# Differential attention in a hybrid layer: prompt scores as two fp32r passes over stacked high and low halves

## The chip, the cores and the metric

One core of a Trainium2 chip runs the kernel. The metric is the device time of one execution in microseconds (us); the time of before is the median of three runs. The profile is one further execution, recorded by the hardware profiler.

## What is computed

One layer on 512 prompt tokens and 64 sample tokens (a second request with a cache of 256 tokens): a gated delta rule (GDN) and a differential attention side by side, then a memory attention, then a feed-forward block. All tensors are fp32. The change touches the differential attention only. Each of its 4 heads has a query and a key of 128 numbers, two components of 64:

```python
s = jnp.einsum('bqhcd,bkhcd->bhcqk', qi.astype(jnp.float32), kf) * scale     # c: the two components
visible = k_pos[None, :] < ((pi // CHUNK + 1) * CHUNK)[:, None]              # chunks of 64
p = jax.nn.softmax(jnp.where(visible, s, -jnp.inf), axis=-1)
a = p[:, :, 0] - lam * p[:, :, 1]
o = jnp.einsum('bhqk,bkhe->bqhe', a, vf)
```

The new keys and values of prompt and sample are outputs too. The GDN works in chunks of 128 tokens (four of the prompt, and a fifth for the sample); for each it inverts a triangular system (`gdn_prep`) and then carries a state through the chunks (`gdn_scan`).

## The kernel before

The layer is kept transposed (features on the 128 partitions, 576 tokens along a row). A projection (`project`, L169) makes 128 output features for all tokens: a first half of 256 prompt tokens and a second half of 256 prompt and 64 sample tokens, each into one PSUM bank of the tag `pr`, of which there are three (L75). Weights and activations stand split into a high and a low fp32r part; a half takes 16 matmuls (8 of 512 columns, 8 of 256) or 24 (of 320 columns). An `evac` function empties the bank, and the bank is free for another half when its last reader is done.

In the order of the program: projections of the GDN, `gdn_prep` of chunk c+1 ahead of `gdn_scan` of chunk c (L905), then for each head h `diff_project(h)` (L946: query, key and value), one step of the sample's scan, and `diff_head(h)` (L996: the sample's tile t = 4 first, then the prompt's tiles 0 to 3). The tile framework's scheduler then orders each engine's instructions by priority and readiness, with buffers handed out as they come free; nothing but that sets the order here. It puts the projections of the attention among the steps of the GDN, and those of the next head among the scores of this one.

`gdn_prep` has a loop of levels (L755): on PE a turn of `Y` and a product of `Dt` and `B` into a bank `g0` or `g1`; ACT copies `X` (L763); DVE makes `Y` (L764); PE multiplies them; DVE updates `Y` (L771) and `Dt` (L772); then the next level. Chunks 0 to 3 have five levels between the first and the last 64 rows, and a closing part (L773 to 784); the sample's chunk 4 has five. `normed` (L798) and the row norms use a power on POOL (`rpow`, L207), for which DVE waits.

Buffers are of tags with one or two slots (`small`, L92). `At0`/`At1` and `Y0`/`Y1` have one slot each and serve the chunks of even and odd number in turn, the sample's chunk 4 those with 0. `kd`, `vb`, `X`, `KQ` and `zr` have two. `zr` is the fp32 buffer into which a projection's bank is emptied.

Of `diff_project`, before: the query's bank is copied into `qz` (L194, L195, L957), component c into its 64 rows of a buffer of its own whose other 64 rows are zero (L942, L943, memsets on POOL); keys go to `kdT` in the large buffer `u5`, transposes of keys and values through a bank `ba` to the output and to `vtm`, in `u5` as well. A score of `diff_head` is one fp32 matmul of `qz[:, c]` (128 columns of queries) against `kdT` (nk = 128, 256, 384 or 512 keys for t = 0 to 3); in the profile each fp32 matmul is two instructions. The SyncE queue (SP) issues all loads and stores in order, weights (`raw`, three slots, L157) among them; an issue that must wait holds those behind it.

Of the kernel before, what the change touches and what calls it, by code (L numbers as in the profile page):

```python
# [8 lines left out]
F32 = mybir.dt.float32  # L9
F32R = mybir.dt.float32r  # L10
AF = mybir.ActivationFunctionType
ALU = mybir.AluOpType
# [3 lines left out]
P = 128  # L16
D = 1024
KT = 8
SEQ = 512
DEC = 64  # L20
T = SEQ + DEC
HALVES = ((0, 256), (256, T - 256))
PAST = 256
# [14 lines left out]
def hybrid_layer_kernel(  # L38
# [9 lines left out]
    nc = tc.nc  # L48
    V, A, G = nc.vector, nc.scalar, nc.gpsimd
# [17 lines left out]
    cp = ctx.enter_context(tc.tile_pool(name="cp", bufs=1))  # L67
# [32 lines left out]
    def bank(tag="ba"):  # L100
        return ps.tile([P, 512], F32, tag=tag, name=nm(tag), bufs=BANKS[tag])
# [4 lines left out]
    def mm(out, lhsT, rhs, start=True, stop=True, pin=False, skip_group_check=False):  # L106
        i = nc.tensor.matmul(out, lhsT, rhs, start=start, stop=stop, skip_group_check=skip_group_check)  # L107
        if pin:
            tc.keep_in_program_order(i)
# [11 lines left out]
    e2, e3, e4, e5 = [pair(i) for i in (2, 3, 4, 5)]  # L121
# [71 lines left out]
    def add_to(dst, b, more):  # L193
        A.copy(dst, more)  # L194
        V.tensor_tensor(dst, b, dst, ALU.add)  # L195
# [244 lines left out]
    for typ in (1, 0, 2):  # L440
# [3 lines left out]
        for h in range(H):  # L444
# [8 lines left out]
            n = SOFF + DEC  # L453
# [40 lines left out]
    for a0, n in HALVES:  # L494
        b = bank("pr")
# [7 lines left out]
    b = bank()  # L503
# [50 lines left out]
    for j in range(3):  # L554
        b = bank()
# [374 lines left out]
    nlam = const([P, 1], "nlam")  # L930
    V.scalar_tensor_tensor(nlam, le[:, 1:2], -LAM0, le[:, 0:1], ALU.add, ALU.subtract)

    od, kdT = e3[:, 0], e5[:, 0]
    vtm = view(e5, 1, 4, 4 * P)
    vs = cp.tile([P, 4, P], F32, tag="vs", name="vs")
    cv2 = view(e3, 1, 4, 4 * P).rearrange("p (i b) n -> p i b n", i=2)
    ckT, cvv = cv2[:, 0].rearrange("p b (c n) -> p (b c) n", n=PAST), cv2[:, 1]

    qz = [cp.tile([P, 2, T], F32, tag=f"qz{i}", name=f"qz{i}") for i in range(2)]
    with tc.issue_after(behind_keys[0]), tc.issue_after(behind_keys[1]):  # L940
        for q2 in qz:
            G.memset(q2[64:, 0, :], 0.0)  # L942
            G.memset(q2[:64, 1, :], 0.0)  # L943
        G.memset(vs[64:], 0.0)

    def diff_project(h):  # L946
        hs = slice(h * P, (h + 1) * P)
        for kind, base in (("q", 2056), ("k", 2568), ("v", 3080)):
            def evac(b, a0, n, more):
                ts_ = slice(a0, a0 + n)  # L950
                if kind == "q":
                    for c in range(2):
                        R = slice(64 * c, 64 * c + 64)
                        if more is not None:
                            add_to(qz[h % 2][R, c, ts_], b[R], more[R])
                        else:
                            (A.copy if c else V.tensor_copy)(qz[h % 2][R, c, ts_], b[R])  # L957
                    return
                d = small("zr", [P, 320])[:, :n] if kind == "v" else kdT[:, h, ts_]
                if more is not None:  # L960
                    add_to(d, b, more)
                else:
                    V.tensor_copy(d, b)
                bt = bank()
                for t in range(2):
                    tr(bt[:, t * P : (t + 1) * P], d[:, t * P : (t + 1) * P])
                if a0:
                    tr(bt[:DEC, 256:384], d[:, 256:])
                src, t2 = bt[:, :256].rearrange("p (t d) -> p t d", t=2), slice(a0 // P, a0 // P + 2)
                if kind == "v":  # L970
                    A.copy(vtm[:, t2, hs], src)
                    if a0:
                        A.copy(vs[:DEC, h, :], bt[:DEC, 256:384])
                else:
                    ko = small("ko", [P, 3, P])
                    A.copy(ko[:, :2], src)
                    nc.sync.dma_start(o_dk_p[0, 0, a0 : a0 + 256, h, :].rearrange("(t p) d -> p t d", p=P), ko[:, :2])
                    if a0:
                        A.copy(ko[:DEC, 2], bt[:DEC, 256:384])
                        nc.sync.dma_start(o_dk_s[0, 0, :, h, :], ko[:DEC, 2])  # L980

            project(weights(w2, base + h * P), xs, evac)
        nc.sync.dma_start(o_dv_p[0, 0, :, h, :].rearrange("(t p) d -> p t d", p=P), vtm[:, :, hs])
        nc.sync.dma_start(o_dv_s[0, 0, :, h, :], vs[:DEC, h, :])

    def diff_cache():
# [9 lines left out]
    def diff_head(h, between):  # L996


        hs = slice(h * P, (h + 1) * P)
        so, co = tiny([P, 5], "ta"), tiny([P, 5], "ta")  # L1000
        on = small("an", [P, 5, P])
        for t in (4, 0, 1, 2, 3):
            if t == 1:
                between()
            q0 = QT[t][0]
            nk = q0 + P if t < 4 else PAST + DEC
            nb = (nk + P - 1) // P
            pr = []
            mx, l = tiny([P, 2], "ta"), tiny([P, 2], "ta")
            for c in range(2):  # L1010
                b = bank(f"g{c}")
                qq = qz[h % 2][:, c, q0 : q0 + P]
                if t < 4:
                    mm(b[:, :nk], qq, kdT[:, h, :nk])
                    V.memset(b[:64, nk - 64 : nk], -1e30)
                else:
                    mm(b[:, :PAST], qq, ckT[:, h, :])
                    mm(b[:, PAST:nk], qq, kdT[:, h, SEQ:T])
# [4 lines left out]
                pr.append(p)  # L1023
# [12 lines left out]
            for kb in range(nb):  # L1036
                if t < 4:
                    vv = vtm[:, kb, hs]
# [41 lines left out]
    for w, out in ((w_mem_k, o_mk), (w_mem_v, o_mv)):  # L1080
        dst = tokens
        for f in range(2):
            fs = slice(512 * f, 512 * f + 512)
            bs = [bank("pr") for _ in range(2)]
            for kc in range(4):
                wt = split_weights(w[0, 256 * kc : 256 * kc + 256, fs], [P, 2, 512])
                for k in (2 * kc, 2 * kc + 1):
                    for t in range(2):
                        ts_ = slice(t * P, (t + 1) * P)
                        for j, (wi, x) in enumerate(((0, mh), (0, ml), (1, mh))):  # L1090
                            mm(
                                bs[t], x[:, k, ts_], wt[wi][:, k % 2, :],
                                start=(k == 0 and j == 0), stop=(k == KT - 1 and j == 2),
# [6 lines left out]
            if out is o_mk:  # L1100
                for i in range(2):
                    b = bank()
# [79 lines left out]
    for k2 in range(KT // 2):  # L1182
        b = bank()
# [6 lines left out]
    for h in range(H):  # L1190
# [15 lines left out]
        for t, (q0, _) in enumerate(QT):  # L1206
            t0, n = TT[t]
            kk, kl = (mkT, mkl) if t < 4 else (cmT, cml)
            b = bank(("gs", "g0", "g1")[t % 3])
# [9 lines left out]
            p = small("p0", [P, 512])  # L1219
# [15 lines left out]
        for i in range(2):  # L1235
            b, b2 = bank(("g0", "gs")[i]), bank(("g1", "ba")[i])
# [8 lines left out]
            j = 2 * (h % 2) + i  # L1245
# [328 lines left out]
    for m in range(KT):  # L1574
# [3 lines left out]
        if m in (3, 4):  # L1578
            t = m - 3
# [43 lines left out]
```

## Time and profile before

| | |
|---|---|
| time, median of 3 runs | 987.23 us (987.15 to 987.32) |
| the profiled execution, its own time | 987.2 us |
| its span in the trace | 985.5 us (1.7 us lie around it) |
| granted TensorE clock, mean | 0.997 |
| PE, DVE, ACT, POOL busy | 98%, 71%, 54%, 6% of the span |
| from chunk 2's second level of the GDN to the end of chunk 4 | 189 to 248 us |
| scores of the differential attention | 250 to 348 us |

PE's busy time counts a matmul from its start to its modelled end, so neighbours overlap; what one costs in a dense stretch is read from start to start, or from the end of one to the end of the next. Names of buffers stand without their numbers in the profile: `g` is a bank g0 or g1, `u` any of the large buffers.

### The profile page before, as it was taken

Reading aid. Unit: us, or ns where it says so; the run is one execution under the profiler, and the core shown is the slowest. Engines: PE = TensorE matmul, PEld = TensorE weight load, DVE = VectorE, ACT = ScalarE, POOL = GpSimd, SP = SyncE. Lnnn points to the kernel's source line nnn. Section 1 sums busy time; section 2 is a strip of 40 time slices with the busy share of each in tenths; the row PEclk is TensorE's granted clock in tenths of the full one; section 3 lists DMA queues with packets and bytes.
Section 4 is the critical chain, followed back from the end, with each engine's and each line's share of the span. In section 5 each row is a group of like instructions: output and inputs, shape, how many; then the busy total and the mean of one; then the engine's idle time right before and its main releaser. Section 6 shows DMA issues by size and latency. Waiting matters only on the chain.

```text
span 985.5 us, 16923 instructions
## 1 busy us (share of the span) xinstructions
PE 968.5 (98%) x6403; PEld 891.2 (90%) x6403; DVE 699.7 (71%) x1570; ACT 530.1 (54%) x1194; POOL 58.8 (6%) x127
## 2 busy tenths in 40 slices
PE   9999999999999999999999999999999999999996
PEld 7989899898888878999999999999999999999996
DVE  6666787877676676666557977657867779978674
ACT  7545575344656665444445657665544445555444
POOL 3341011101000000000000000000000000000000
PEclk9999999999999999999999999999999999999998
DMA  7432340103222647333111414222222223223202
GB/s 212 129 119 65 90 138 23 43 23 103 81 68 68 203 131 227 95 94 99 44 44 58 127 54 127 86 86 86 86 87 86 86 86 86 86 86 86 65 23 96
DMA packets 121714, 90.75 MB, mean 92 GB/s; under 512 B 5564, under 2 KB 112206, under 8 KB 121122
## 3 DMA queue, kind: packets, MB, share of 16 engines
q1 hardware_dynamic: 121266, 89.03, 30.9%
q8 instruction: 50, 0.82, 0.3%
q10 hardware_dynamic: 368, 0.66, 0.2%
q14 instruction: 30, 0.25, 0.1%
HBM read 79.93 MB, written 9.75 MB: 91 GB/s over the span
## 4 chain that ended last, share of the span: by engine, by line
PE 83%; DVE 4%; issue 3%; POOL 2%; DMA 2%; ACT 2%; POOLq 0%; ACTq 0%; SPq 0%; DVEq 0%
PE pr L107 51%; PE g L107 12%; PE ba L107 10%; PE gs L107 6%; PE ba L113 3%; PE g L113 1%; POOL tg L208 1%; DMA r<-in_w_ff_dram 1%; DVE p L457 1%; DVE wl L162 0%; DMA grow<-gdram 0%; DMA raw<-in_w_ff_dram 0%; POOL X L607 0%; POOL X L608 0%; DVE on L809 0%
## 5 line engine op out<-in xcount | busy, mean ns | idle before, releaser
L107 PE MATMUL pr<-u,wh 128*128 128x320 f32 (+2 forms) x1240 | 328.7, 343 | 1.3 <-DVE p L323 1.2
L107 PEld LDWEIGHTS pr<-u,wh 128*128 128x128 f32 x1240 | 212.3, 188 | 18.0 <-DVE p L323 1.8
L107 PE MATMUL pr<-u,wl 128*128 128x256 f32 (+1 forms) x816 | 226.7, 302 | 0.0
L107 PEld LDWEIGHTS pr<-u,wl 128*128 128x128 f32 x816 | 149.9, 189 | 2.7 <-DVE wl L388 0.2
L162 DVE TENSOR_TENSOR wl<-raw,wh 128x1024 fp32r<-128x1024 f32 x65 | 79.4, 1223 | 41.3 <-ACT wh L161 41.0
L161 ACT CAST wh<-raw 128x1024 fp32r<-128x1024 f32 x65 | 68.1, 1048 | 65.7 <-PE pr L107 50.5
L107 PE MATMUL pr<-u,w2h 128*128 128x320 f32 (+1 forms) x384 | 98.5, 340 | 0.0
L1369 ACT CAST w2h<-r 128x512 fp32r<-128x512 f32 x56 | 34.7, 620 | 87.9 <-PE pr L107 85.3
L107 PE MATMUL pr<-f,w2h 128*128 128x320 f32 (+1 forms) x288 | 74.3, 340 | 0.1
L107 PEld LDWEIGHTS pr<-u,w2h 128*128 128x128 f32 x384 | 65.0, 188 | 4.5 <-ACT u L1452 0.3
L107 PE MATMUL pr<-u,w2l 128*128 128x256 f32 (+1 forms) x256 | 65.1, 295 | 0.0
L1454 DVE TENSOR_TENSOR u<-u,pr 128x256 f32<-128x256 f32 x96 | 42.3, 448 | 16.9 <-PE pr L107 16.2
L107 PE MATMUL ba<-u,wl 128*128 128x288 f32 x360 | 53.0, 296 | 0.4 <-ACT keep L1405 0.4
L107 PEld LDWEIGHTS pr<-f,w2h 128*128 128x128 f32 x288 | 48.7, 188 | 4.0 <-issue 1.1
L107 PEld LDWEIGHTS ba<-u,wl 128*128 128x128 f32 x360 | 49.2, 188 | 1.2 <-ACT keep L1405 1.1
L107 PE MATMUL pr<-f,w2l 128*128 128x256 f32 (+1 forms) x192 | 48.8, 295 | 0.0
L107 PEld LDWEIGHTS pr<-u,w2l 128*128 128x128 f32 x256 | 46.9, 188 | 1.5
L208 POOL TENSOR_TENSOR tiny<-tiny,nhalf 128x1 f32<-128x1 f32 (+4 forms) x10 | 8.7, 870 | 631.6 <-DVE tiny L1522 529.8
L1370 DVE TENSOR_TENSOR w2l<-r,w2h 128x512 fp32r<-128x512 f32 x56 | 38.5, 688 | 10.7 <-ACT w2h L1369 10.4
L107 PE MATMUL pr<-wh,u 128*128 128x512 f32 x128 | 41.4, 401 | 0.0
L1414 ACT ACTIVATE c<-c 128x288 f32<-128x288 f32 x48 | 20.6, 443 | 29.5 <-DVE c L1413 29.5
L107 PEld LDWEIGHTS pr<-f,w2l 128*128 128x128 f32 x192 | 35.2, 188 | 1.2
(514 smaller groups left out, 2025.1 us busy)
## 6 DMA issues: line engine op xcount, KB each, us to landing
raw<-in_w_ff_dram SPq DMA_DIRECT2D x36, 512.0 KB
raw<-in_w_in_dram SPq DMA_DIRECT2D x28, 512.0 KB
r<-in_w_ff_dram SPq DMA_DIRECT2D x56, 256.0 KB
raw<-in_w_mem_k_dram SPq DMA_DIRECT2D x8, 512.0 KB
raw<-in_w_mem_v_dram SPq DMA_DIRECT2D x8, 512.0 KB
raw<-in_w_out_dram SPq DMA_DIRECT2D x8, 512.0 KB
raw<-in_w_mem_q_dram SPq DMA_DIRECT2D x8, 512.0 KB
raw<-in_w_mem_o_dram SPq DMA_DIRECT2D x8, 512.0 KB
```

What stands on the lines that cost most here:

```text
L107: i = nc.tensor.matmul(out, lhsT, rhs, start=start, stop=stop, skip_group_check=skip_group_check)
L113: i = nc.tensor.transpose(out, in_, ident[:n, :n])
L161: A.copy(wh, raw)
L162: V.tensor_tensor(wl, raw, wh.bitcast(F32), ALU.subtract)
L208: G.tensor_tensor(out, in_, bc(nhalf[: in_.shape[0], 0:1], list(in_.shape)), ALU.pow)
L457: V.scalar_tensor_tensor(yv[:, :n], cb[:, i : i + n], cwt[:, m, i : i + 1], yv[:, :n], ALU.mult, ALU.add)
L1369: A.copy(wh, src)
L1370: V.tensor_tensor(wl, src, wh.bitcast(F32), ALU.subtract)
L1414: A.activation(c, c, AF.Relu)
L1454: V.tensor_tensor(am, am, b, ALU.add)
```

## The change

The query and the key of a prompt score are split into a high and a low fp32r part. For each component the query's high part (64 rows) stands over its low part (64 rows) in one buffer `qs[:, c]` of 128 rows; the key's high part stands in both halves of one buffer, and its low part in both halves of another. Two fp32r matmuls into the same bank give all four products. The sample's scores stay fp32 with zero rows.

The parts are made on the partitions on which the projection leaves them: `qn` (tags `At0`, `At1`) and `kn` (in `u5`, kept for two heads) by an ACT cast and a DVE subtraction for each half, and the SyncE queue then moves 64 rows to where they belong: four moves for the query (L972, 128 KB each), two of 256 KB for component 1 of the key (L988), and one of 256 KB for component 0, which overwrites what those two have read (L989). The large buffer `u5` thereby has no room for `vtm`, which becomes four tiles of the tags `kd`, `vb`, `X`, `KQ`; the sample's zero-padded query `qz` and its new keys stand in `Y0` and `Y1`; values go out in four stores instead of one. Component 1 is computed before component 0.

```diff
-    od, kdT = e3[:, 0], e5[:, 0]
-    vtm = view(e5, 1, 4, 4 * P)
+    od = e3[:, 0]
+    kdu = pair(5, F32R)
+    vtm = [small(tag, [P, 4 * P]) for tag in ("kd", "vb", "X", "KQ")]
...
-    qz = [cp.tile([P, 2, T], F32, tag=f"qz{i}", name=f"qz{i}") for i in range(2)]
+    qs = [cp.tile([P, 2, T], F32R, tag=f"qz{i}", name=nm("qs")) for i in range(2)]
+    qy = [small(f"Y{i}", [P, 4 * P]) for i in range(2)]
+    qz, knew = [y[:, : 2 * P].rearrange("p (c n) -> p c n", c=2) for y in qy], [y[:, 2 * P : 2 * P + DEC] for y in qy]
...
+    def kd_of(h):
+        return kdu[:, h % 2].rearrange("p (c j) t -> p c j t", c=2)
+
     def diff_project(h):
         hs = slice(h * P, (h + 1) * P)
+        qn = [small(tag, [P, SEQ], dt=F32R) for tag in ("At0", "At1")]
+        kn = kd_of(h)[:, 0]
...
                 if kind == "q":
-                    for c in range(2):
-                        R = slice(64 * c, 64 * c + 64)
-                        if more is not None:
-                            add_to(qz[h % 2][R, c, ts_], b[R], more[R])
-                        else:
-                            (A.copy if c else V.tensor_copy)(qz[h % 2][R, c, ts_], b[R])
+                    d = b
+                    if more is not None:
+                        d = small("zr", [P, 320])[:, :n]
+                        add_to(d, b, more)
+                    A.copy(qn[0][:, ts_], d[:, :n0])
+                    V.tensor_tensor(qn[1][:, ts_], d[:, :n0], qn[0][:, ts_].bitcast(F32), ALU.subtract)
+                    if a0:
+                        for c in range(2):
+                            R = slice(64 * c, 64 * c + 64)
+                            A.copy(qz[h % 2][R, c, :], d[R, n - P :])
+                            for j in range(2):
+                                nc.sync.dma_start(
+                                    qs[h % 2][64 * j : 64 * j + 64, c, :SEQ].bitcast(F32), qn[j][R].bitcast(F32)
+                                )
                     return
-                d = small("zr", [P, 320])[:, :n] if kind == "v" else kdT[:, h, ts_]
+                d = small("zr", [P, 320])[:, :n]
...
+                if kind == "k":
+                    A.copy(kn[:, 0, ts_], d[:, :n0])
+                    V.tensor_tensor(kn[:, 1, ts_], d[:, :n0], kn[:, 0, ts_].bitcast(F32), ALU.subtract)
+                    if a0:
+                        A.copy(knew[h % 2], d[:, 256:])
+                        k0, k1 = (kd_of(h)[:, c, :, :SEQ].bitcast(F32) for c in range(2))
+                        for j in range(2):
+                            nc.sync.dma_start(k1[64 * j : 64 * j + 64], k0[64:])
+                        nc.sync.dma_start(k0[64:], k0[:64])
...
-            for c in range(2):
+            for c in (1, 0):
                 b = bank(f"g{c}")
-                qq = qz[h % 2][:, c, q0 : q0 + P]
                 if t < 4:
-                    mm(b[:, :nk], qq, kdT[:, h, :nk])
+                    for j in range(2):
+                        mm(b[:, :nk], qs[h % 2][:, c, q0 : q0 + P], kd_of(h)[:, c, j, :nk], start=j == 0, stop=j == 1)
```

The scheduler orders the program anew. Three places of its order follow, each in the names of the built program (a buffer with its number).

PE around the end of chunk 2's levels, before: `pr_2729` is the second half of head 0's value, and `g_313` to `g_318` are chunk 2's levels.

```order
L107 MATMUL pr_2729<-u_93,wh_2701 128x320
L107 MATMUL g_313_2039<-Y_304_2003,X_2002 128x128 x2
L113 MATMUL g_341_2167<-ident,u_78 128x128 x4
L107 MATMUL pr_2729<-u_93,wh_2701 128x320
L107 MATMUL pr_2729<-u_93,wl_2702 128x320
L107 MATMUL pr_2729<-u_93,wh_2701 128x320 x2
L107 MATMUL pr_2729<-u_93,wl_2702 128x320
L107 MATMUL g_345_2186<-u_75 128x128
L113 MATMUL g_315_2047<-ident,Y_304_2003 128x128 x2
```

The same place of the change: `pr_2731` is the first half of head 0's value.

```order
L107 MATMUL pr_2731<-u_94,wh_2727 128x512
L107 MATMUL g_313_2039<-Y_304_2003,X_2002 128x128 x2
L113 MATMUL g_341_2167<-ident,u_78 128x128 x4
L107 MATMUL g_345_2186<-u_75 128x128
L113 MATMUL g_315_2047<-ident,Y_304_2003 128x128 x2
L107 MATMUL g_315_2047<-Dt_305_2004,B_314_2045 128x128 x2
L113 MATMUL gs_2149<-ident,on_2139 128x128 x4
L107 MATMUL g_345_2186<-u_75 128x128 x3
```

No matmul into `pr` stands between `g_313` and chunk 4's fourth level any more; the next one, `pr_2756`, stands behind its `g_422`, and the first of the query of head 1, `pr_3002`, behind `g_426`, the end of chunk 4.

ACT in the change, in chunk 4's levels: `At_398` is the chunk's own matrix in the slot `At0`, `At_451` the high part of head 0's query in the same slot, `pr_2616` the bank of that query's second half.

```order
L757 COPY B_423_2484<-At_398_2403 128x128
L965 CAST At_451_2586<-zr_2611 128x256
L965 CAST At_451_2586<-pr_2616 128x256
L1003 COPY p_465_2680<-ba_2677 128x256
L770 COPY Y_407_2426<-Dt_408_2427 128x4x16
L763 COPY X_2425<-g_421_2474 128x128
```

Before, the copies that empty the query's bank (L194, L957) stood in front of `gdn_prep` of chunk 3; they now stand behind the last use of the slot by chunk 4.

SP in the change, behind the key of head 0: `u_2571` holds the key's parts, `kd_2572` to `KQ_2575` are the four tiles of `vtm`.

```order
L157 DMA raw_3471<-in_w_in_dram 128x8x128
L988 DMA u_2571<-u_2571 64x2x512 x2
L1011 DMA out_dram<-kd_2572 128x128
L1011 DMA out_dram<-vb_2573 128x128
L1011 DMA out_dram<-X_2574 128x128
L1011 DMA out_dram<-KQ_2575 128x128
L989 DMA u_2571<-u_2571 64x2x512
L1012 DMA out_dram<-vs 64x128
```

The key's last move stands behind the four stores of the value; before, no move stood there, and the values went out in one store.

More of the change, by code (lines that the diff above doesn't have):

```diff
@@ L944, in hybrid_layer_kernel @@
         G.memset(vs[64:], 0.0)
+    def kd_of(h):
+        return kdu[:, h % 2].rearrange("p (c j) t -> p c j t", c=2)
     def diff_project(h):
         hs = slice(h * P, (h + 1) * P)
+        qn = [small(tag, [P, SEQ], dt=F32R) for tag in ("At0", "At1")]
+        kn = kd_of(h)[:, 0]
         for kind, base in (("q", 2056), ("k", 2568), ("v", 3080)):
             def evac(b, a0, n, more):
-                ts_ = slice(a0, a0 + n)
+                ts_ = slice(a0, min(a0 + n, SEQ))
+                n0 = ts_.stop - a0
                 if kind == "q":
-                    for c in range(2):
-                        R = slice(64 * c, 64 * c + 64)
-                        if more is not None:
-                            add_to(qz[h % 2][R, c, ts_], b[R], more[R])
-                        else:
-                            (A.copy if c else V.tensor_copy)(qz[h % 2][R, c, ts_], b[R])
+                    d = b
[12 more added lines that the diff above has]
+                                )
                     return
-                d = small("zr", [P, 320])[:, :n] if kind == "v" else kdT[:, h, ts_]
+                d = small("zr", [P, 320])[:, :n]
                 if more is not None:
@@ L970, in evac @@
                 if kind == "v":
-                    A.copy(vtm[:, t2, hs], src)
+                    for t in range(2):
+                        A.copy(vtm[a0 // P + t][:, hs], src[:, t])
                     if a0:
@@ L982, in diff_project @@
             project(weights(w2, base + h * P), xs, evac)
-        nc.sync.dma_start(o_dv_p[0, 0, :, h, :].rearrange("(t p) d -> p t d", p=P), vtm[:, :, hs])
+        for t in range(4):
+            nc.sync.dma_start(o_dv_p[0, 0, t * P : (t + 1) * P, h, :], vtm[t][:, hs])
         nc.sync.dma_start(o_dv_s[0, 0, :, h, :], vs[:DEC, h, :])
@@ L1007, in diff_head @@
             nb = (nk + P - 1) // P
-            pr = []
+            pr = {}
             mx, l = tiny([P, 2], "ta"), tiny([P, 2], "ta")
-            for c in range(2):
+            for c in (1, 0):
                 b = bank(f"g{c}")
-                qq = qz[h % 2][:, c, q0 : q0 + P]
                 if t < 4:
-                    mm(b[:, :nk], qq, kdT[:, h, :nk])
+                    for j in range(2):
+                        mm(b[:, :nk], qs[h % 2][:, c, q0 : q0 + P], kd_of(h)[:, c, j, :nk], start=j == 0, stop=j == 1)
                     V.memset(b[:64, nk - 64 : nk], -1e30)
                 else:
-                    mm(b[:, :PAST], qq, ckT[:, h, :])
-                    mm(b[:, PAST:nk], qq, kdT[:, h, SEQ:T])
+                    mm(b[:, :PAST], qz[h % 2][:, c, :], ckT[:, h, :])
+                    mm(b[:, PAST:nk], qz[h % 2][:, c, :], knew[h % 2])
                 V.tensor_reduce(mx[:, c : c + 1], b[:, :nk], AX.X, ALU.max)
@@ L1022, in diff_head @@
                 A.activation(p[:, :nk], b[:, :nk], AF.Exp, bias=mx[:, c : c + 1], scale=0.125, accum_out=l[:, c : c + 1])
-                pr.append(p)
+                pr[c] = p
             V.reciprocal(l, l)
@@ L1037, in diff_head @@
                 if t < 4:
-                    vv = vtm[:, kb, hs]
+                    vv = vtm[kb][:, hs]
                 else:
```

## The prediction

> **What bounds the kernel now.** I read the page first, for the engines and the chain that ended last, then the stretches of time around the change, then single rows there (start and duration in us).
>
> ```profile
> PE 968.5 (98%) x6403; PEld 891.2 (90%) x6403; DVE 699.7 (71%) x1570; ACT 530.1 (54%) x1194; POOL 58.8 (6%) x127
> PE 83%; DVE 4%; issue 3%; POOL 2%; DMA 2%; ACT 2%; POOLq 0%; ACTq 0%; SPq 0%; DVEq 0%
> ```
>
> PE is busy 98% and holds 83% of the chain. So a microsecond of matmul saved in a dense stretch is a microsecond gained, and a microsecond of PE waiting is one lost, unless other matmuls fill it. Two stretches matter: the GDN's last part, where projections of the attention are the filling, and the attention itself. The rows of the view by windows give the length and then busy time of PE, its weight loads, DVE, ACT and POOL, and behind them the granted clock.
>
> ```profile
> 189.10:248.30 59.20, 56.94 (x437) 52.02 (x436) 44.15 (x124) 25.24 (x66) 6.44 (x8) 1.00 0.25 66
> 250.00:358.00 108.00, 107.05 (x631) 88.87 (x630) 74.82 (x241) 65.07 (x210) 4.78 (x7) 1.00 0.34 104
> ```
>
> PE idles 2.3 us in 59.2 and 1.0 us in 108. DVE and ACT have 33 and 43 us to spare in the second.
>
> **The change, part by part.** First the **scores**. In a dense stretch a matmul costs the time from one end to the next.
>
> ```profile
> 318.19 0.38 PE L113 MATMUL ba<-ident,p 128*128 128x128 f32 x2
> 318.41 1.02 PE L107 MATMUL g<-u,qz 128*128 128x512 f32 x2
> ...
> 332.91 0.40 PE L107 MATMUL pr<-wl,u 128*128 128x512 f32 x1
> 333.14 0.62 PE L107 MATMUL pr<-wh,u 128*128 128x512 f32 x2
> ...
> 253.42 0.28 PE L107 MATMUL pr<-u,wl 128*128 128x256 f32 x1
> 253.54 0.40 PE L107 MATMUL pr<-u,wh 128*128 128x512 f32 x1
> ...
> 261.50 0.28 PE L107 MATMUL pr<-u,wl 128*128 128x256 f32 x1
> 261.61 0.86 PE L107 MATMUL g<-u,qz 128*128 128x384 f32 x2
> ```
>
> The fp32 score of 512 keys is two instructions and ends at 319.43, the row before at 318.57: 0.86 us. An fp32r pass of 512 starts and ends 0.23 after another (332.91 to 333.14, and two more end at 333.76, 0.45 after 333.31), one of 256 columns takes 0.12 (253.42 to 253.54). So 512 keys go from 0.86 to 0.46; 384 keys from 0.69 (261.78 to 262.47) to 0.35, with a pass halfway between 0.12 and 0.23; 256 keys from 0.43 (half of 0.86) to 0.24. For 128 keys the fp32 score is 0.22 by the same proportion. An fp32r pass so narrow stands nowhere in the trace: between 0.06 by width and 0.22, were each pass as dear as the fp32 score it halves; I take 0.12, that of 256 columns, the nearest row, so 0.24 for two. Sum for one component of a head: -0.40 - 0.34 - 0.19 + 0.02 = -0.91 (-1.03 to -0.71), for eight **-7.3 us** (-8.2 to -5.7).
>
> Then the **moved projections**, the larger term. Head 0's query is now emptied by casts into the slots `At0` and `At1`, which chunk 4 and chunk 3 of the GDN hold until their levels are done; its second half stays in its bank meanwhile, its first half in `zr`, and the second `zr` holds the key. So three banks fill up (query, key, value) and PE has no projection to place: the order of the change shows none from `g_313` to behind `g_422`. What stood there before:
>
> ```profile
> L107 PE MATMUL pr<-u,wh x77: 303/312/476, 188.8 to 247.3; 128*128 128x320 f32 x53, 128*128 128x512 f32 x24
> L107 PE MATMUL pr<-u,wl x51: 277/309/411, 189.0 to 248.1; 128*128 128x320 f32 x27, 128*128 128x256 f32 x24
> ...
> 317.60 0.46 PE L107 MATMUL pr<-u,wh 128*128 128x320 f32 x2
> 317.89 0.46 PE L107 MATMUL pr<-u,wl 128*128 128x320 f32 x2
> ```
>
> Two of 320 columns take 0.29 (317.60 to 317.89), so 80 x 0.146 + 24 x 0.23 + 24 x 0.12 = 20.1 us. Seven of the half-projection's matmuls that stood just ahead are put off as well (1.0 us), and 24 stand in the stretch's end still (`pr_2756`, 3.5 us): 20.1 + 1.0 - 3.5 = 17.6 us of matmuls go behind the stretch, where PE is full. The change therefore loses what the stretch does not get shorter by: 17.6 less (59.2 - X), with X its new length. It breaks even within itself at X = 41.6.
>
> X depends on what holds the levels up. One level of chunk 3, from its product `g<-Dt,B` to the next:
>
> ```profile
> 208.35 0.62 PE L107 MATMUL g<-Dt,B 128*128 128x128 f32 x4
> 209.01 0.37 ACT L763 COPY X<-g 128x256 f32<-128x256 f32 x1
> 209.41 0.42 DVE L764 SCALAR_TENSOR_TENSOR Y<-lev,g 128x256 f32<-128x256 f32 x1 [0.81 <-ACT X L763]
> 209.89 0.71 PE L107 MATMUL g<-Y,X 128*128 128x128 f32 x4
> 210.64 0.29 DVE L771 TENSOR_TENSOR Y<-Dt,g 128x128 f32<-128x128 f32 x1
> 210.96 0.42 DVE L772 TENSOR_TENSOR Dt<-Dt,g 128x256 f32<-128x256 f32 x1
> 211.78 0.28 PE L107 MATMUL g<-Dt,B 128*128 128x128 f32 x1
> ```
>
> It takes 3.4 us, of which 2.8 are the six steps themselves. Hardly a projection stands in it: the level is a chain through three engines, and taking projections out does not shorten it. Another level:
>
> ```profile
> 216.82 0.42 DVE L764 SCALAR_TENSOR_TENSOR Y<-lev,g 128x256 f32<-128x256 f32 x1 [0.40 <-ACT X L763]
> 217.30 0.71 PE L107 MATMUL g<-Y,X 128*128 128x128 f32 x4
> 218.51 0.16 DVE L807 TENSOR_TENSOR tg<-tg,tg 128x4 f32<-128x4 f32 x1 [0.86 <-POOL tg L208]
> 218.71 0.69 DVE L809 TENSOR_TENSOR on<-gs,tg 128x512 f32<-128x512 f32 x1
> 219.32 0.28 DVE L771 TENSOR_TENSOR Y<-Dt,g 128x128 f32<-128x128 f32 x1
> ```
>
> Here `Y` was ready at 218.0 by PE and is made at 219.3, because DVE, in order, waits for POOL's power ahead of it. That is the GDN's own too. In the order of the change DVE meets such waits at other levels, as often. I went through the stretch step by step and counted only the time in which a projection's matmul, copy or weight subtraction stood ahead: 1.7 us in the rest of chunk 2 and 1.4 because chunk 3's first level comes ahead of chunk 2's last product; 0.6 in chunk 3 with its changed waits; 0.9 between chunks 3 and 4; 2.2 in chunk 4, where a 1.2 us weight subtraction and a copy of a bank stood before `Y` and `Dt`. Together 6.8, so X = 52.4 and the loss is 17.6 - 6.8 = **+10.8 us**. Ends: X no shorter (59.2) gives +17.6; every level at its 2.8 plus 0.3 for six handoffs, 2.2 in chunk 4 with its half-sized steps, and the closing parts bare gives X = 42.5 and +0.9. I take the value between because both levels shown run above the bare chain for reasons that stay.
>
> At the **joint** behind chunk 4 ACT has a queue of casts and copies ahead of what frees the query's bank, and head 1's query must wait for it.
>
> ```profile
> 244.83 1.66 ACT L201 CAST u<-u 128x512 fp32r<-128x512 f32 x3
> 246.55 0.63 ACT L201 CAST u<-u 128x512 fp32r<-128x512 f32 x1
> ```
>
> These four (2.3 us) now stand together ahead of chunk 4's last copy; 1.6 us of `pr_2756` cover part: **+1.2 us**, between 0 and 3.3 (2.3 and two copies of 0.5).
>
> **Copies.**
>
> ```profile
> L194 ACT COPY qz<-pr x8: 366/367/370, 148.5 to 300.5; 64x256 f32<-64x256 f32 x8
> L195 DVE TENSOR_TENSOR qz<-pr,qz x8: 398/422/429, 149.3 to 301.0; 64x256 f32<-64x256 f32 x8
> L957 DVE COPY qz<-pr x4: 472/479/483, 159.5 to 307.6; 64x320 f32<-64x320 f32 x4
> L957 ACT COPY qz<-pr x4: 419/421/421, 161.0 to 309.1; 64x320 f32<-64x320 f32 x4
> ...
> L1199 ACT CAST kd<-zr x4: 402/405/406, 465.9 to 519.0; 128x256 fp32r<-128x256 f32 x4
> L1200 DVE TENSOR_TENSOR ql<-zr,kd x4: 418/422/425, 466.5 to 519.4; 128x256 fp32r<-128x256 f32 x4
> ```
>
> Per head ACT loses 2 x 0.37 + 0.42 and gains one copy of 0.37, four casts of 0.41 and three small copies (under 0.3 each): about +1.7; DVE loses 2 x 0.42 + 0.48 and gains 0.42 + 4 x 0.42: about +0.8. In all +7 and +3 us, beside 43 and 33 idle ones; taken as 0, at most +7 should ACT become the bound there.
>
> **The moves.** Seven issues a head on SP, and three more stores. Component 1 needs one hop, component 0 two in a row, with the stores between. No move within the core's memory stands in the trace; the nearest rows are in the chain of waits:
>
> ```profile
> 118.45 1.24 DMA gdram<-p
> 119.77 4.02 DMA grow<-gdram
> ```
>
> 10 KB took 1.24, 256 KB 4.02. Two hops are 2.5 to 8.0 us; I take 8.0. The order puts between head 1's first value transposes, which release the stores, and its first score of component 0 about 7.9 us of PE (21 projection matmuls, 3.5; the sample's scan, 3.0; the scores of tile 4, 1.1; transposes, 0.3), and the first hop is on its way before. So 0, up to +2 a head, 8 in all. [...]
>
> **Sum**: the profiled execution's 987.2 (span 985.5 and 1.7 around it; the median is 987.23, the same) - 7.3 + 10.8 + 1.2 = **991.9 us**.
>
> **The rivals.** (a) The bare chain: without projections the levels run near their floor. Decisive is X: below 59.2 - 17.6 + 7.3 - 1.2 = 47.7 the kernel is faster. At X = 45 it is 987.2 - 7.3 + 3.4 + 1.2 = 984.5. For it: DVE is busy 44 of 59 us of which projections had 7 (3.5 of copies from `pr`, three subtractions of 1.2); against it: the 37 that stay, and the level of 3.4 us with no filling in it. (b) The moves come late: SP holds the key's first move behind two weight loads, and weights in the chain took 6.15 (the row below); 6.15 + 4.02 against 7.9 is +2.3 a head: 1001.
>
> ```profile
> 590.91 6.15 DMA r<-in_w_ff_dram
> 193.00:197.00 4.00, 2.75 (x23) 2.55 (x22) 2.63 (x13) 0.30 (x1) 1.64 (x1) 1.00 0.16 48
> ```
>
> (c) The two passes save nothing at the widths of 128 and 256 and little above, so the scores give 2 instead of 7.3: 997. (d) The clock: in the second row above PE was busy 2.75 of 4 us and the granted clock stayed 1.00; should it fall to half in the thinned stretch, the GDN's 37 us of PE (56.9 - 20.1) would take 74, X about 75: 1015. [...]
>
> **How the numbers follow.** The forecast (988.5 to 996.5, X within 4 us of 52.4) has 0.58, (a) 0.21 (982 to 987), (b) 0.10, (c) 0.07, (d) 0.04. A measurement here tells about 0.2% (2 us) from no change. Faster by more is half of (a) and a rest of the forecast's: 0.14. Within is the other half and the forecast's lower end: 0.15. Slower: 0.71. The range, 984.5 to 999, leaves out part of (a), (b) and (d).
>
> **What would show it.** Right: PE idle for 10 us or more between 189 and 245, next to no `pr` matmuls there, chunk 4's end near 241 instead of 248, `qn` casts just before it, `pr` dense behind it; scores of 512 keys at 0.46. Wrong: levels at 3.0 us (then (a)); PE waiting for a DMA at `g<-u,qs` (then (b)); a granted clock under 1 there (then (d)).

## The result and the profile after

The changed kernel takes **998.18 us** (median of 4 runs, 996.58 to 1002.34), the kernel before 987.28 beside it: ratio 1.0117, 95% interval 1.0086 to 1.0147. It is slower by 10.9 us where 4.7 were forecast: 6.3 us above the number and above the band named for the forecast itself (988.5 to 996.5), inside the range (984.5 to 999) by 0.8 us. The profiled execution is the slowest of the four: 1002.34, span 1000.6.

On the page of the changed kernel, the engines, PE's granted clock in 40 slices of 25 us (tenths), and the chain that ended last:

```profile
PE 970.0 (97%) x6403; PEld 893.2 (89%) x6403; DVE 700.9 (70%) x1578; ACT 534.5 (53%) x1222; POOL 57.1 (6%) x127
...
PEclk9999999998999999999999999999999999999999
...
PE 61%; DVE 3%; DMA 2%; issue 2%; ACT 2%; POOLq 0%; POOL 0%; ACTq 0%; SPq 0%; DVEq 0%
```

PE works as long as before (970.0 against 968.5 us) in a span 15.1 us longer, and the tenth slice, 225 to 250 us, shows a granted clock below 0.9, which no slice of the kernel before did ahead of its last one. Both point at the GDN's last part. By the windows of the changed kernel (length, then busy time of PE, PEld, DVE, ACT, POOL, and behind them clock, DMA share, GB/s), first the same stretch up to chunk 4's last transposes, then pieces of its end:

```profile
190.60:246.10 55.50, 44.32 (x315) 38.42 (x316) 37.84 (x117) 20.58 (x58) 7.17 (x12) 0.94 0.14 40
...
235.00:238.40 3.40, 1.61 (x9) 0.96 (x7) 2.70 (x13) 1.44 (x6) 1.01 (x1) 0.97 0.39 90
238.40:245.00 6.60, 6.00 (x26) 5.92 (x26) 3.64 (x10) 2.52 (x7) 0.00 (x0) 0.50 0.64 179
245.00:250.00 5.00, 5.00 (x32) 4.63 (x31) 4.05 (x8) 3.06 (x8) 0.49 (x3) 1.00 0.48 181
```

Before, PE idled 2.3 us in the stretch; now it idles 11.2 (55.50 - 44.32). And where PE is busy again, it runs at a granted clock of 0.50 for 6.8 us (238.2 to 245.0). What projection work is left, by the tile `pr` of the changed kernel in that stretch, and PE's waits there:

```profile
L107 PE MATMUL pr<-u,wh x14: 309/468/615, 239.6 to 245.9; 128*128 128x320 f32 x14
...
L107 PE MATMUL pr<-u,wl x6: 309/468/468, 240.2 to 245.6; 128*128 128x320 f32 x6
```

```profile
PE g L107 <- DVE Y L764: 3.2, 6, 1.1
PE g L113 <- DVE Dt L772: 1.1, 2, 0.9
PE g L113 <- DVE tg L805: 1.1, 1, 1.1
```

128 projection matmuls have become some 20, all behind 239 us, and PE waits for the levels' own steps on DVE. The median durations of 468 against 312 ns before are that clock seen in single rows: all 13 of 320 columns between 239.6 and 244.4 us take 468 to 615 ns, the `wl` one at 245.19, where the clock is 1.00 again, 0.31 us.

The scores, in the changed kernel's timeline around 297 us and 287 us:

```profile
297.71 0.39 PE L107 MATMUL pr<-u,wh 128*128 128x512 f32 x1
297.94 0.51 PE L107 MATMUL g<-u,qs 128*128 128x384 f32 x2
298.29 0.40 PE L107 MATMUL pr<-u,wl 128*128 128x256 f32 x2
298.52 0.40 PE L107 MATMUL pr<-u,wh 128*128 128x512 f32 x1
298.76 0.62 PE L107 MATMUL g<-u,qs 128*128 128x512 f32 x2
```

```profile
286.83 0.28 PE L107 MATMUL pr<-u,wl 128*128 128x256 f32 x1
286.95 0.33 PE L107 MATMUL g<-u,qs 128*128 128x128 f32 x2
```

From end to end: 512 keys 298.92 to 299.38, 0.46; 384 keys 298.10 to 298.45, 0.35; 128 keys 287.11 to 287.28, 0.17. These are the forecast's prices (0.46, 0.35, 0.24), the narrowest cheaper in this row.

How far the kernel is behind at two later places is read from one group of rows, the low parts of the last weights on DVE, which stand at 588.8 and 938.2 us (first and last start) in the kernel before. The kernel before and the changed kernel:

```profile
L1370 DVE TENSOR_TENSOR w2l<-r,w2h x56: 678/688/693, 588.8 to 938.2; 128x512 fp32r<-128x512 f32 x56
```

```profile
L1398 DVE TENSOR_TENSOR w2l<-r,w2h x56: 680/685/693, 600.7 to 953.3; 128x512 fp32r<-128x512 f32 x56
```

It is 11.9 us late ahead of the feed-forward stage and 15.1 behind it. So 3.2 us of this execution were lost where the change has no instruction.

### The profile page after: what moved, and what is told of

Same layout as the page of the kernel before. It is cut to its first block, busy times and chain, and to the rows that moved or that the text cites. A ratio compares the mean times of both kernels' runs of the same rounds, so it can differ in the third digit from the quotient of the medians.

```text
span 1000.6 us, 17054 instructions
## 1 busy us (share of the span) xinstructions
PE 970.0 (97%) x6403; PEld 893.2 (89%) x6403; DVE 700.9 (70%) x1578; ACT 534.5 (53%) x1222; POOL 57.1 (6%) x127
## 4 chain that ended last, share of the span: by engine, by line
PE 61%; DVE 3%; DMA 2%; issue 2%; ACT 2%; POOLq 0%; POOL 0%; ACTq 0%; SPq 0%; DVEq 0%
PE pr L107 40%; PE ba L107 9%; PE g L107 6%; PE gs L107 4%; PE ba L113 2%; DMA raw<-in_w_ff_dram 2%; DMA r<-in_w_ff_dram 1%; ACT c L1443 0%; ACT c L1442 0%; DVE w L1297 0%; DVE s L1342 0%; DVE u L1490 0%; DVE w2l L1398 0%; DVE raw L1347 0%; DVE wl L1297 0%
## 5 line engine op out<-in xcount | busy, mean ns | idle before, releaser
L1398 DVE TENSOR_TENSOR w2l<-r,w2h 128x512 fp32r<-128x512 f32 x56 | 38.5, 687 | 10.4 <-ACT w2h L1397 10.2
```

Source lines behind the costliest of these rows:

```text
L1398: V.tensor_tensor(wl, src, wh.bitcast(F32), ALU.subtract)
```

## The experiments

The theories: **A**, the projections that cannot be placed cost about 11 us, the scores give back up to 7, and a fall of the clock behind the thinned stretch adds a few; **B**, the added casts, copies and moves cost; **C**, the clock is the whole loss. Where an edit concerns scores in fp32, the key's low part is left out of them.

### The changed kernel again

No edit.

> The changed kernel once more, nothing edited, for a second profile and more times. Theory A (the projections that head 0's held slots push out of the last part of the GDN cost about 11 us, the scores give 7.6 back, and a fall of the granted clock behind the thinned stretch costs about 3 more in those executions that have it): 996 to 999, executions with a mean clock near 0.994 about 3 us above those near 0.998, and in the profile next to no projection matmul between 190 and 238 us. Theory C (the granted clock is the whole loss): an execution with the clock of the kernel before, 0.997, takes 990 or less. If the 3.4 us that the first profile lost behind 480 us to weights arriving late belong to the kernel, they stand in this profile too; if they are chance, not.

Measured: 999.64 us (997.07 to 1001.24, 4 runs), ratio 1.0122 (1.0106 to 1.0137). The mean clocks of its executions sort its times: 0.996 with 997.07 and 998.70, 0.990 with 1000.59 and 1001.24. The profiled one (997.07) in windows:

```profile
189.00:242.90 53.90, 42.89 (x315) 36.78 (x315) 37.32 (x116) 20.03 (x58) 7.17 (x12) 0.97 0.11 32
233.00:236.30 3.30, 1.62 (x12) 1.04 (x10) 3.12 (x13) 1.88 (x8) 0.51 (x1) 1.00 0.26 60
236.30:239.60 3.30, 2.79 (x11) 2.42 (x12) 2.03 (x7) 0.53 (x2) 0.50 (x1) 0.51 0.80 218
```

```profile
L1398 DVE TENSOR_TENSOR w2l<-r,w2h x56: 681/689/694, 597.8 to 948.1; 128x512 fp32r<-128x512 f32 x56
```

Here the clock of 0.50 lasted 3.4 us, half as long, and the stretch is 53.9 long instead of 55.5. An estimate of what each fall cost is half of PE's busy time in it, 3.0 us (of 6.00) and 1.4 (of 2.79); without it both stretches are 52.5 long. This execution is 9.0 late ahead of the feed-forward stage and 9.9 behind it. So of the 3.2 us lost there in the first profile 0.9 came again and 2.3 did not. Theory C falls too: the execution with the highest clock of all eight, 0.998, which is that of the kernel before (0.997 to 0.998), took 996.58 us and so is still 9.3 us slower.

### Only the query's slots freed

```diff
-        qn = [small(tag, [P, SEQ], dt=F32R) for tag in ("At0", "At1")]
+        if h:
+            qn = [small(tag, [P, SEQ], dt=F32R) for tag in ("At0", "At1")]
+        else:
+            qn = [qs[1][:, j, :SEQ] for j in range(2)]
```

> Head 0's query casts go to a buffer that is free (that of head 1's stacked query) instead of the slots held by the GDN's last chunks; everything else as changed. By its order 4 more projection matmuls stand ahead of the GDN's end (820 against 816; 927 before the change). Theory A, with the loss in proportion to the projections put off: 996 to 998, hardly better, since the key's buffers and the slots of the sample's query block next. The prediction's own wording, that the query's slots are what empties the banks: 988 to 992. Theory B (the loss is in the casts, copies and moves that were added): 996 to 998 as well.

Measured: 998.60 us (996.11 to 998.97), ratio 1.0108 (1.0094 to 1.0122): nothing gained. The prediction named the query's slots as what fills the banks; that was too narrow. With them free, the sample's query (slots `Y0` and `Y1`), the key's tile in `u5` and the two `zr` buffers hold the next half projections in the same way; which of them holds how much is read from the program and was not tried one by one. In this execution the clock fell to 0.50 twice, for 3.4 us at 218.6 and for 10.2 at 239.1; the longer fall and the piece ahead of it, by windows:

```profile
234.80:238.80 4.00, 2.66 (x20) 1.96 (x19) 3.25 (x13) 2.38 (x9) 0.76 (x1) 1.00 0.23 65
238.80:249.20 10.40, 8.39 (x27) 6.51 (x28) 7.43 (x17) 4.35 (x12) 0.81 (x4) 0.52 0.52 166
```

### The stretch filled again

The casts' slots as above; the sample's query and new key of head 0 in a free buffer (`an`), and the key emptied into rows of `od`, which are free until its head's output. The second run adds a third `zr`.

```diff
-    qy = [small(f"Y{i}", [P, 4 * P]) for i in range(2)]
+    qy = [small("an", [P, 5 * P])] + [small(f"Y{1 - h % 2}", [P, 4 * P]) for h in (1, 2)]
+    qy.append(qy[1])
...
-                d = small("zr", [P, 320])[:, :n]
+                d = small("zr", [P, 320])[:, :n] if kind == "v" else od[:, h, a0 : a0 + n]
...
-        bufs = 1 if tag in ("vn", "on", "S") or tag[:-1] in ("At", "Dt", "Y") else 2
+        bufs = 1 if tag in ("vn", "on", "S") or tag[:-1] in ("At", "Dt", "Y") else 3 if tag == "zr" else 2
```

> Head 0's casts, sample query and new key go to buffers that are free, and the key is emptied into the rows that later hold its head's output instead of the two rotating buffers: all casts, copies, moves and two-pass scores stay. By its order 912 projection matmuls stand ahead of the GDN's end (816 in the changed kernel, 927 before). Theory A: the loss goes but for 15 matmuls (2.2 us): 987.2 - 7.6 + 2.2 + up to 2 of copies = 982 (979.5 to 985), clock as before the change. Theory B (casts, copies and moves cost): 995 or more. Theory C (clock): 994 to 996.

> As the run filled, with a third of the rotating 128 x 320 buffers. By its order 936 projection matmuls stand ahead of the GDN's end, 9 more than before the change. Theory A: 987.2 - 7.6 = 980 (977.5 to 982.5), some 2 us below the run filled. Theory B: 995 or more, no better than the run filled. Theory C: 994 to 996.

Measured: 986.32 us (11 runs), ratio 0.9988 (0.9979 to 0.9997), and with the third buffer 983.12 (981.83 to 984.43), ratio **0.9956** (0.9943 to 0.9968). All casts, copies, moves and two-pass scores are still there, and 12 to 16 us of loss are gone: B falls, A stands. The windows of the second:

```profile
189.00:247.20 58.20, 57.53 (x444) 53.16 (x443) 43.73 (x125) 25.92 (x73) 7.17 (x12) 1.00 0.22 56
250.00:370.00 120.00, 116.85 (x698) 98.83 (x699) 85.50 (x260) 75.14 (x239) 5.80 (x8) 1.00 0.58 164
```

PE idles 0.7 us in the stretch, less than the 2.3 before the change, and the clock stays at 1.00. But both runs are 3 to 4 us above what A expected, outside its ranges, and in the attention PE now idles 3.2 us, where it idled 1.8 in the same 120 us before the change. Its longest wait there:

```profile
PE ba L113 <- DMA p<-in_cache_diff_k_dram: 1.7, 1, 1.7
```

### The banks held, nothing else

The kernel before, with three half projections of head 0 copied through slots that chunk 4 holds; fp32 scores, no casts, no moves.

```diff
+    HELD = {("q", 256): "At0", ("k", 256): "Dt0", ("v", 0): "Y0"}
...
+                if h == 0 and (kind, a0) in HELD:
+                    held = small(HELD[kind, a0], [P, 4 * P])[:, :n]
+                    if more is not None:
+                        add_to(held, b, more)
+                        more = None
+                    else:
+                        A.copy(held, b)
+                    b = held
```

> The kernel before the change, its fp32 scores and buffers as they were, but three of head 0's half projections (the query's second, the key's second, the value's first) are emptied into the slots At0, Dt0 and Y0 that the GDN's last chunk holds, and copied on from there. No casts, no moves, no two passes. By its order 820 projection matmuls stand ahead of the GDN's end (816 in the changed kernel, 927 in the kernel before). Theory A: the held banks alone cost what the changed kernel lost in that place, 11 to 13, and about 3 more in executions with a lower clock: 998 to 1003. Theory B (casts, copies, moves): 988 to 989.

Measured: 1002.71 us (1000.89 to 1003.22, 5 runs), ratio 1.0151 (1.0137 to 1.0165). The execution with the highest clock, 0.998, took 1000.89, that with the lowest, 0.992, 1003.22. Its profile repeats the changed kernel's:

```profile
189.50:242.40 52.90, 43.95 (x320) 37.66 (x321) 36.46 (x113) 19.59 (x54) 6.27 (x7) 0.97 0.09 27
213.60:217.60 4.00, 2.12 (x12) 1.42 (x12) 3.08 (x11) 1.06 (x5) 1.01 (x1) 0.94 0.01 2
217.60:220.80 3.20, 3.02 (x15) 3.03 (x16) 2.54 (x9) 0.33 (x1) 0.00 (x0) 0.54 0.00 0
```

```profile
PE pr L107 <- ACT Dt L959: 2.1, 1, 2.1
```

The held banks alone lose 15.5 us, at the upper end of what A gave; 2.1 us of it are a wait that only this kernel has, for its own copy into `Dt0`. As its scores are fp32, it compares with the changed kernel with fp32 scores (below, 1004.77), which is 17.5 above the kernel before: 13.4 of these 17.5 are the held banks'. So they make most of the loss; the other 4 us they do not show. At the two places read above it is 15.1 and 15.5 us late:

```profile
L1380 DVE TENSOR_TENSOR w2l<-r,w2h x56: 683/691/693, 603.9 to 953.7; 128x512 fp32r<-128x512 f32 x56
```

### What the scores are worth in time

```diff
-                    for j in range(2):
-                        mm(b[:, :nk], qs[h % 2][:, c, q0 : q0 + P], kd_of(h)[:, c, j, :nk], start=j == 0, stop=j == 1)
+                    mm(b[:, :nk], qs[h % 2][:, c, q0 : q0 + P].bitcast(F32), kd_of(h)[:, c, 0, :nk].bitcast(F32))
```

In the kernel with the filled stretch and the third buffer:

> The run filled3 with its two-pass scores replaced by one fp32 product of the stacked query and the key's high part; the key's low part is left out of the scores. Casts, copies and moves all stay. Theory A: the scores lose what they gave, +7.6 us on the run filled3: 990.7 (989 to 992), that is some 3.5 above the kernel before, which is then the price of casts, copies and moves together. If the two passes gave less than the rows say (the prediction's rival c), +2 to +4: 985 to 987.

Measured: 987.12 us (11 runs), ratio to the kernel before 1.0002 (0.9993 to 1.0011). So the scores are worth **4.0 us** there, between the two expectations, and casts, copies and moves together cost nothing in the end. That is a net figure: by the low parts of the last weights this kernel is 1.3 us ahead of the kernel before at the feed-forward stage (587.5 against 588.8) and level with it behind that stage (938.3 against 938.2). One of PE's waits is shorter with the longer scores, 0.6 instead of 1.7 us:

```profile
PE ba L113 <- DMA p<-in_cache_diff_k_dram: 0.6, 1, 0.6
```

In the changed kernel itself:

> The changed kernel with its two-pass scores replaced by one fp32 product of the stacked query and the key's high part; the key's low part is left out of the scores. The run filled3_fp32 showed that the scores are worth 4.0 us of time where the stretch is filled, though their rows differ by 6.9. If the rest is lost to waits of the softmax chain there, here, where more projections are left over to stand between the scores, nearly all 7 should show: 1004 to 1007. If the scores are worth 4 in every setting: 1002 to 1004.

Measured: 1004.77 us (1002.72 to 1006.08), ratio 1.0176 (1.0161 to 1.0190): 5.1 above the repeated run, 6.6 above the first. Its profiled execution and the repeated one's have the same mean clock, 0.996, and compare place by place:

```profile
L1397 DVE TENSOR_TENSOR w2l<-r,w2h x56: 683/690/693, 603.0 to 953.8; 128x512 fp32r<-128x512 f32 x56
```

5.2 us behind the repeated run's 597.8, 5.7 behind its 948.1. The two settings do not give the same, and neither gives the 7 of the rows. The difference of 4.0 and 5 to 6 is not far above the scatter.

### The wait for the cache

```diff
+        if h == 0:
+            diff_cache()
         diff_project(h)
         next(sample, None)
-        if h == 0:
-            diff_cache()
```

> The run filled3 with the loads and transposes of the attention's cache written ahead of head 0's projections, so that the loads do not stand behind the moves in SyncE's queue. In the run filled3 PE waited 1.7 us for such a load at 249 us. By its order 930 projection matmuls stand ahead of the GDN's end (936 in filled3). If that wait is the moves' doing and nothing takes its place: 981 to 982.5. If the softmax chain is late at the same place anyway: 983 to 984.

Measured: **981.56 us** (981.32 to 982.75, 5 runs), ratio 0.9944 (0.9932 to 0.9957), the fastest kernel of the study. The load's wait is gone from PE's waits and nothing of its size took its place; 1.6 us were won. By the two rows above, 1.1 us of the scores' saving had gone into this wait.

### The moves doubled

Every move of the filled kernel (third buffer) issued twice; the query's are shown, the key's are doubled likewise.

```diff
                             for j in range(2):
-                                nc.sync.dma_start(
-                                    qs[h % 2][64 * j : 64 * j + 64, c, :SEQ].bitcast(F32), qn[j][R].bitcast(F32)
-                                )
+                                for _ in range(2):
+                                    nc.sync.dma_start(
+                                        qs[h % 2][64 * j : 64 * j + 64, c, :SEQ].bitcast(F32), qn[j][R].bitcast(F32)
+                                    )
```

> The run filled3 with every move on the SyncE queue issued twice, 14 a head instead of 7. If the moves are hidden (the prediction's term of 0): 982 to 985, as the run filled3. If they stand on the path as the prediction's rival b has it, the second set costs what the first did: +2.3 a head, 992; a loss of 1 to 2 would be the wait of the cache's load behind them in SyncE's queue, once, at head 0.

Measured: 988.91 us (987.19 to 990.13, 11 runs), 5.8 above the single set: neither expectation. PE waits for no move in this profile. Its waits between 280 and 300 us, and two windows there:

```profile
PE ba L113 <- DVE p L1061: 0.9, 1, 0.9
PE gs L107 <- ACT aT L1068: 0.7, 2, 0.4
PE g L107 <- ACT p L1056: 0.6, 1, 0.6
```

```profile
284.50:288.50 4.00, 2.47 (x18) 1.99 (x16) 3.06 (x10) 1.52 (x8) 0.00 (x0) 0.98 0.79 183
288.50:291.50 3.00, 2.68 (x13) 2.42 (x12) 0.42 (x1) 1.39 (x6) 0.09 (x1) 0.50 0.70 154
```

With later moves, 24 more projection matmuls stand ahead of the first score (1006 against 982 in the order), so fewer are left to stand between head 0's scores; there PE waits for the softmax on DVE and ACT, and the clock falls to 0.50 after that. The price of late operands is paid in cover, not in a wait for the DMA. That explanation is read from one profile and was not tried by itself.

### PE kept busy in the levels

The changed kernel with transposes that feed nothing.

```diff
+            if c == 4:
+                for j in (1, 3):
+                    for _ in range(2):
+                        tr(b[:, j * P : (j + 1) * P], ident)
...
+            if c > 1:
+                for j in (2, 3, 2, 3):
+                    tr(bx_bank[:, j * P : (j + 1) * P], ident)
```

> The changed kernel with extra transposes of the identity into unused columns of the banks of the levels: four (0.11 us each) behind the second product of each level of the GDN's chunks 2 to 4, four more behind the first in chunk 4. They feed nothing. The casts still wait for the held slots and 820 projection matmuls stand ahead of the GDN's end (816 in the changed kernel). If the fall of the granted clock comes from the thinned stretch, the mean clock goes to 0.997 in every execution, and the times come close together at 994 to 997, the transposes themselves costing up to 2 of the 3 us won. If the clock falls for another reason, it stays between 0.990 and 0.998 and the times between 996 and 1001. In both cases the loss to the put-off projections stays: nothing under 993.

Measured: 1001.73 us (1000.22 to 1002.05, 4 runs), ratio 1.0141 (1.0126 to 1.0157). The mean clock is 0.997 or 0.998 in all four executions, against 0.990 to 0.998 without the transposes. In the profile the stretch has no fall:

```profile
190.00:246.00 56.00, 47.51 (x376) 41.82 (x376) 39.29 (x116) 20.69 (x60) 5.88 (x9) 1.00 0.11 31
...
L113 PE MATMUL g<-ident 128*128 128x128 f32 x68 | 10.4, 272 | 0.0
```

So the fall does come from the thinned stretch. As a cure it was worth nothing: the 68 transposes in this window, at 0.11 us each (four end to end from 212.55 to 212.99), are 7.5 us, and standing ahead of the levels' next products they cost more than the clock did. My "up to 2" took them as hidden.

## Why the prediction was right, and where it was short

The direction and the main cause were right; the change came out more than twice as large as forecast.

**The scores** were priced right as a difference: 19.35 us of score matmuls (own tiles, without the sample) became 11.95 when I add the end-to-end times of all rows, the idle time just ahead of them included: -7.4. There is some luck in it: the forecast's prices give 17.6 and 10.3, both too low by 1.7. The step that failed is that the sum counted PE's saving as time. In time the scores are worth 4.0 (filled stretch) to 5 or 6 (changed kernel). The reason seen in part: with shorter scores PE comes sooner to what it then waits for, 1.1 us of it the cache's load. The rest was not settled.

**The moved projections** were right to a few tenths. The forecast was X = 52.4 and a loss of 10.8; without the fall of the clock the two profiles give 52.5, by the estimate above, and a loss of 10.9. Chunk 4's end was to come near 241: with the fall taken off it came at 241.5 in the repeated run (242.9 - 1.4), and at 243.1 in the first profile, whose stretch began 1.5 us late. PE idle of 10 us or more (11.2), no `pr` matmul until 238 or 239, the levels waiting for DVE: all there. The runs with the stretch filled again and with the banks alone held show it as the main cause. Only which slots hold was put too narrowly.

**The clock** is the other step that failed. The prediction bounded it by one window, 2.75 of 4 us busy at a clock of 1.00, and set a fall for the whole stretch (rival d, 1015, chance 0.04) against none; its own sign for (d), a clock under 1 there, came in a smaller form. That the clock would fall to half was (d)'s assumption; the falls measured are to 0.50. What happened lies between: falls to 0.50 of 3.4, 6.8 or 10.2 us behind a few us in which PE was busy for only a part of the time (1.61 of 3.40; 1.62 of 3.30; 2.12 of 4.00; ahead of the longest, in the run with only the query's slots freed, 2.66 of 4.00). That last share is hardly below the 2.75 of 4 of the prediction's row, so one such row could not bound the clock. The falls come more or less often from one execution to the next: the one with a clock of 0.998 took 996.58, those with 0.990 took 1000.59 and 1001.24, so they cost up to 4 or 5 us, and 1.6 at the median (998.18 - 996.58). A term of about +2 was missing. The changed kernel scatters over 6 us where the kernel before scatters by 0.4 to 2.9.

**The joint** was +1.2. The changed kernel's windows behind the stretch:

```profile
250.00:255.00 5.00, 4.31 (x28) 3.42 (x28) 2.45 (x7) 2.93 (x10) 0.00 (x0) 1.00 0.88 206
255.00:260.00 5.00, 4.95 (x34) 4.48 (x33) 2.97 (x10) 2.73 (x7) 0.00 (x0) 1.00 0.54 118
```

0.7 us idle, of which 0.6 is one wait, the same in both profiles of the changed kernel:

```profile
PE ba L113 <- DVE zr L195: 0.6, 1, 0.6
```

So the size is near, but the mechanism is not the forecast's: PE waits here for an addition on DVE, not behind ACT's casts, and from 246.1 to 250 it idles nothing. **Copies and moves** at 0: confirmed as a net by the filled kernel with fp32 scores, 987.12 against 987.28.

The sum with what was measured, without a fall of the clock: 987.2 - 5.5 (scores) + 10.9 (17.6 less 6.7) + 0.7 (joint) + 1 (feed-forward) = 994.3. The execution whose clock shows no fall took 996.58, so 2.3 us stand in no term. Of the 6.3 us between forecast and result, then, about 2 are the scores, 1 the feed-forward stage, 1.6 the clock, and the rest, some 2 us, no run places.

The feed-forward part stays open. Between the two places read above, the kernels with moves lost 0.7 to 3.2 us more than the kernel before, the kernel with held banks and no moves 0.4. The chain of waits of the changed kernel has weights in it late in that stage that it did not have there before the change, in its first profile and in its second:

```profile
877.14 5.39 DMA raw<-in_w_ff_dram
```

```profile
872.54 4.86 DMA raw<-in_w_ff_dram
```

But the kernel with held banks and no moves has such a row as well (4.02 us at 830.86), so the row alone does not show the loss. Why they come late was not tried.

## What to carry to other kernels

Ask of every new buffer who holds it at the moment of its first use: a cast into a slot that an earlier stage still owns keeps its PSUM bank, and a few such banks stop all the filling work, which here cost more than the faster matmuls gave. Freeing one of the holders did nothing while the next ones held as well (998.6); freeing them together, with a third `zr`, turned a loss of 10.9 us into a gain of 4.2 (983.12), and the cache's loads moved ahead made it 5.7 (981.56). Where a busy engine is thinned, look at its clock behind the gap too (0.50 for 3.4 to 10.2 us here), and count a saving on the bounding engine as time only as far as its next operands are there.

## What the runs showed of the hardware

PE's granted clock fell to 0.50 without a real pause: the longest single wait in the changed kernel's stretch was 1.1 us, where the kernel before kept its clock at 1.00 behind a wait of 1.3 (between 193 and 197 us).

Leaving out the last 7 us of each execution, the falls read in windows were all to 0.50. They lasted 6.8 us in the changed kernel, 3.4 in the repeated run, 3.4 and 10.2 with only the query's slots freed, 3.4 with the banks alone held and 3.4 with the moves doubled. What sets their length was not tried. Not every thin piece brought a fall, as this window of the changed kernel shows:

```profile
199.40:202.80 3.40, 1.56 (x13) 1.18 (x11) 3.40 (x8) 0.52 (x2) 0.00 (x0) 1.00 0.00 0
```

PE was as little busy here as ahead of the fall (1.56 against 1.61 of 3.40), and the clock stayed at 1.00. So the busy share of such a piece does not decide it alone. What else counts stays open.

The fall hit what followed: 6.00 of 6.60 us were busy behind 238.4, at a clock of 0.50.

Two fp32r passes of 128 columns take 0.17 us from end to end in the row shown, and 0.20 as a mean over the changed kernel's first profile, against 0.24 in the forecast.
